# Weight sums of the branches' product pairs: from DRAM sums to VectorE sums in a two-layer recurrent trunk

## The chip, the cores and the metric

The kernel runs on one core of a Trainium2 chip. The metric is the device time of one execution in microseconds (us), the median of the runs taken. The engines that matter here are TensorE (PE in the profile, with its weight loads as PEld), VectorE (DVE), ScalarE (ACT), GpSimd (POOL) and SyncE (SP). SP only issues DMAs; ACT and POOL issue DMAs beside their arithmetic.

## The reference

The reference is a trunk of two layers over 512 frames of width 1024, all in float32. Each layer normalises x, projects it to about 12,300 columns, runs two branches (an mLSTM with four heads and a multi-scale retention with four heads, both chunkwise-recurrent), merges them under two sigmoid gates, and then adds a feed-forward block with a squared ReLU and a gated per-layer embedding. Cut to what the change touches:

```python
h = rmsnorm(x, norm1_g[i]);  z = h @ w_in[i] + b_in[i]     # q,k,v,o,i,f | rq,rk,rv,rg | gm,gr
rq4 = rope(rq, cos, sin);  rk4 = rope(rk, cos, sin) * R_DK ** -0.5
hr  = retention_chunkwise(rq4, rk4, rv, log_gamma)
y_r = silu(rg) * head_layernorm(hr)
merged = sigmoid(gm) * (y_m @ w_bm[i]) + sigmoid(gr) * (y_r @ w_br[i])
x = x + merged @ w_out[i]
x = x + square(relu(rmsnorm(x) @ w_ff1[i] + b_ff1[i])) @ w_ff2[i] + b_ff2[i]
x = x + sigmoid(rmsnorm(x) @ w_pe_gate[i]) * (p[i] @ w_pe[i])
```

## The kernel before

**Tiling.** Activations lie transposed in SBUF, 128 features by 512 frames to a tile. Every float32 operand is split into a high and a low part (`split`, L281 and L282: ScalarE writes the high part, VectorE subtracts it to get the low part), and TensorE multiplies high by high, high by low and low by high. A weight must therefore be loaded by SP, then pass through ScalarE, then through VectorE, before TensorE can use it.

**Units.** The work on weights is a fixed list of 314 units for the two layers (`unit_list`). 222 of them are whole: one 128x1024 block of weights of 512 KB, 24 matmuls of 512 columns. The other 92 are pairs (`PAIR`), which compute two output tiles by a seven-product scheme of the Strassen-Winograd kind in place of eight products: `P1` to `P7`, 12 matmuls of 256 columns each, run in the order P1, P5, P2, P6, P3, P7, and P4 only after the next unit has begun (`later`, `flush`). 22 pairs of a layer lie in the branches (rotary q and k, the gates rg, gr, and half of gm), 24 in the feed-forward block.

**Pieces of a pair.** A pair's weights are four quarters B11, B12, B21, B22 (128x512 each, 256 KB, given in `wpairs`) and four sums: t1 = B12 + B11, t3 = B12 + B22, t2 = t1 + B22 (three weights), t4 = t2 + B21 (four weights). They are loaded and split as four pieces: A = (B11, t1), B = (B21, t2), C = (B22, t3), D = (t4), the first three 128x1024, the last 128x512. A is used by P1 and P5, B by P2 and P6, C by P3 and P7, D by P4.

**Sums.** In this version the sums are all made in DRAM before they are needed. The pairs are grouped (24 groups, of four or two pairs), and each group has eight steps: for each of the four sums a DMA that copies the first addend, then a DMA that accumulates the second (`step`, L319, on POOL's queue; 1 MB a step for a group of four). There are 192 steps. `pace` gives each step a unit number from estimated unit times and four intervals in microseconds; `next_unit` issues all steps that are due when a unit begins, and each step carries a dependency on the last matmul written so far, so that it isn't issued before TensorE gets there.

**Loads.** SP loads the raw pieces (tile `wr`, L344 for pairs, L346 for whole units) into four buffers (`RAWS`), in the order in which they are used, about three pieces ahead. A buffer is free again when the piece in it is split. The split pieces A, B, C and the whole units share three pairs of buffers (tag `w`), D has a pair of its own, so a split waits as well until TensorE is done with an older piece. Program order is the priority; the framework's scheduler orders the instructions of each engine at build time by its own estimate of when each is ready, and each engine then runs its list strictly in order. A DMA that depends on nothing is put near the start of its engine's list.

**Evacuation.** The products of a pair accumulate in three PSUM banks (a, b, c). P6, P7 and P4 go on in bank a after ScalarE or VectorE have read what is there (`pair_tiles`, L446 after P1, L448 after P5, L452 after P6, L454 and L456 by VectorE after P3 and P7), and P3 goes on in bank c after L448. These reads stand in the same in-order lists as the splits.

**Rotation tables.** The cosine and sine tables (128x512 each) are loaded on ScalarE's queue (L1062), written in the program after the values of retention head 0, and used first by the rotary step of that head (L917 to L919), after four more units.

Of the kernel before, what the change touches and what calls it, by code (L numbers as in the profile page):

```python
# [38 lines left out]
OP = mybir.AluOpType  # L39
SYNC = mybir.DependencyInfo(mybir.DependencyClass.Sync, mybir.DependencyReason.DATA)  # L40
# [20 lines left out]

HALVED = (1, 2)

EVERY = (16.0, 7.2, 9.8, 11.3)


CQ, CK, CV, CO, CI, CF = 0, 1024, 2048, 3072, 4096, 4100
CRQ, CRK, CRV, CRG, CGM, CGR = 4104, 5128, 6152, 8200, 10248, 11272
# [25 lines left out]

PIECE = {"A": ("B11", "t1"), "B": ("B21", "t2"), "C": ("B22", "t3"), "D": ("t4",)}

GIVEN = ("B11", "B12", "B21", "B22")
MADE = {"t1": ("B12", "B11"), "t3": ("B12", "B22"), "t2": ("t1", "B22"), "t4": ("t2", "B21")}

READY = {"P1": 2, "P4": 2, "P5": 3, "P2": 4, "P6": 4, "P3": 5, "P7": 5}  # L100


def split_steps(k):

    return min(k + 1, 1), min(k, 48), min(max(k - 48, 0), 48), max(k - 96, 0)


def pace(units):

    at, t = [], 0.0  # L110
    for n, u in enumerate(units):
        while len(at) < 8 * len(groups()) and t >= sum(k * e for k, e in zip(split_steps(len(at)), EVERY)):
            at.append(n)
        t += 9.9 if u[0] == "PAIR" else 5.4
    return at


def groups():


    g = {}
    for i in range(L):
        def rqk(h):
            return [("w_in", 0, c + k * 256) for k in (h, h + 1) for c in (CRQ, CRK)]

        def rg(h):
            return [("w_in", 0, CRG + h * 512 + 256 * p) for p in range(4)]
# [103 lines left out]
def build(ctx, tc, ins, out):  # L231
# [1 line left out]
    ve, ac, gp, te = nc.vector, nc.scalar, nc.gpsimd, nc.tensor  # L233
    units = [u for i in range(L) for u in unit_list(i)]
    NU = len(units)
    due = pace(units)

    def pool(name, bufs, **kw):
        return ctx.enter_context(tc.tile_pool(name=name, bufs=bufs, **kw))
# [46 lines left out]
    for g, v in groups().items():  # L286
        index[g] = len(index)
        for x in GIVEN:
            given[g, x] = ins["wpairs"][k:k + len(v)]
            k += len(v)  # L290
        for x in MADE:
            sums[g, x] = tc.dram_tile([len(v), P, Q], F32, name=f"s{index[g]}{x}")

    def block(g, x):
# [5 lines left out]
    def sum_steps():  # L300

        first = lambda g: [(g, "t1", 0), (g, "t3", 0), (g, "t1", 1), (g, "t3", 1)]
        second = lambda g: [(g, "t2", 0), (g, "t2", 1), (g, "t4", 0), (g, "t4", 1)]
        gs = list(index)
        out = first(gs[0])
        for a, b in zip(gs, gs[1:]):
            for x, y in zip(second(a), first(b)):
                out += [x, y]
        return out + second(gs[-1])

    steps = sum_steps()
# [11 lines left out]
    def next_unit():  # L323
        n = at["unit"]
        at["unit"] += 1
        while at["step"] < len(steps) and due[at["step"]] <= n:
            step()
        return n


    order = [(n, x) for n, u in enumerate(units) for x in (PIECE if u[0] == "PAIR" else (0,))]
    place = {x: k for k, x in enumerate(order)}
    raws, pieces = {}, {}
    at = {"unit": 0, "prep": 0, "load": 0, "whole": 0, "step": 0}

    def fill_raws(most=RAWS):
        while at["load"] < len(order) and len(raws) < most:
            n, x = order[at["load"]]
            raws[n, x] = r = wpool.tile([P, UN], F32, name=f"wr{at['load']}", tag="wr", bufs=RAWS)
            if x:  # L340
                _, g, p = units[n]
                assert made[g] == 8, (g, made[g], at["unit"])
                for k, y in enumerate(PIECE[x]):
                    nc.sync.dma_start(r[:, k * Q:(k + 1) * Q], block(g, y)[p])  # L344
            else:
                nc.sync.dma_start(r, ins["wstream"][at["whole"]])  # L346
                at["whole"] += 1
            at["load"] += 1

    def prep_next():  # L350
        n, x = order[at["prep"]]
        at["prep"] += 1
        fill_raws()

        w = Q if x == "D" else UN
        pl = cur["last"] if n >= NU - LAST else wpool
        kw = {"tag": "d", "bufs": 2} if x == "D" else {"tag": "l", "bufs": 2 * LAST} if pl is not wpool else {
            "tag": "w", "bufs": 2 * PIECES}
        out_ = [pl.tile([P, w], F32R, name=f"w{a}{n}_{x}", **kw) for a in "hl"]
        split(raws.pop((n, x))[:, :w], *out_)  # L360
        pieces[n, x] = out_

    def ready(k):
# [414 lines left out]
    for i in range(L):  # L778
# [280 lines left out]

        trig = [cur["low"].tile([P, T], F32, name=f"l{i}{n}", tag="trig", bufs=2) for n in ("cos", "sin")]  # L1060
        for t, n in zip(trig, ("cos", "sin")):
            nc.scalar.dma_start(t, ins[n])  # L1062

        def bm_tile(c):
            if c < 4:
# [287 lines left out]
    cur["last"].release()  # L1353
    n3_pool.release()
    x_pool.release()
    assert at["unit"] == NU and at["prep"] == len(order) and not pieces and not raws and at["load"] == len(order) and at["step"] == len(steps)

# [110 lines left out]
```

## Time and profile before

| | us |
|---|---|
| runs | 2395.94, 2393.9, 2385.51 (median 2393.9) |
| the profiled execution | 2386.71 |
| its span, first to last instruction | 2385.0 |
| TensorE busy | 2344.7 |
| VectorE busy | 1654.2 |
| ScalarE busy | 1257.3 |
| GpSimd busy | 278.3 |

The granted TensorE clock is 0.995 over the span. The DMA queues moved 519.75 MB, of which 192.95 MB on POOL's queue. To read the profile: a group's line gives its source line, engine, operation, written and read tiles, count, busy time, mean duration in ns, and the idle time of the engine just before it with what ended it. In the list of waits, each line names who waited for whom and the total, the count and the longest in us. In the table of stretches each engine has its busy time and, in brackets, its instructions; the last three columns are the granted clock, the DMA engines' busy share and the GB/s that they moved. In the listing by time, the square brackets hold the idle time before the instruction and what ended it.

### The profile page before, as it was taken

Reading aid. Unit: us, or ns where it says so; the run is one execution under the profiler, and the core shown is the slowest. Engines: PE = TensorE matmul, PEld = TensorE weight load, DVE = VectorE, ACT = ScalarE, POOL = GpSimd, SP = SyncE. Lnnn points to the kernel's source line nnn. Section 1 sums busy time; section 2 is a strip of 40 time slices with the busy share of each in tenths; the row PEclk is TensorE's granted clock in tenths of the full one; section 3 lists DMA queues with packets and bytes.
Section 4 is the critical chain, followed back from the end, with each engine's and each line's share of the span. In section 5 each row is a group of like instructions: output and inputs, shape, how many; then the busy total and the mean of one; then the engine's idle time right before and its main releaser. Section 6 shows DMA issues by size and latency. Waiting matters only on the chain. (4 is left out here: it accounts for less than half of the span.)

```text
span 2385.0 us, 37288 instructions
## 1 busy us (share of the span) xinstructions
PE 2344.7 (98%) x14364; PEld 2099.3 (88%) x14364; DVE 1654.2 (69%) x2585; ACT 1257.3 (53%) x1864; POOL 278.3 (12%) x400
## 2 busy tenths in 40 slices
PE   9999989999999999999999999999999999999997
PEld 7788888998998899999887888898989888999996
DVE  6877466774666777777778775676737577777775
ACT  4765344553454656556547563444526456556563
POOL 3111101000001200001311110000000011000011
PEclk9999999999999999999999999999999999999998
DMA  7667799779799788977765567867786887895551
GB/s 227 172 195 197 216 272 261 248 203 268 198 282 301 231 262 235 285 229 220 209 192 141 178 163 225 247 193 205 211 248 188 276 251 214 271 246 184 174 158 42
DMA packets 197811, 519.75 MB, mean 218 GB/s; under 512 B 19313, under 2 KB 21745, under 8 KB 197633
## 3 DMA queue, kind: packets, MB, share of 16 engines
q1 hardware_dynamic: 130032, 292.84, 36.1%
q0 software_dynamic: 50176, 192.95, 34.5%
q10 hardware_dynamic: 17424, 31.59, 3.7%
q8 instruction: 112, 1.84, 0.3%
q14 instruction: 67, 0.54, 0.1%
HBM read 502.62 MB, written 207.62 MB: 298 GB/s over the span
## 5 line engine op out<-in xcount | busy, mean ns | idle before, releaser
L282 DVE TENSOR_TENSOR wl<-wr,wh 128x1024 fp32r<-128x1024 f32 x222 | 272.0, 1226 | 145.4 <-ACT wh L281 144.8
L281 ACT ACTIVATE wh<-wr 128x1024 fp32r<-128x1024 f32 x222 | 234.2, 1057 | 259.2 <-PE l0br L375 30.2
L281 ACT ACTIVATE wh_C<-wr 128x1024 fp32r<-128x1024 f32 x92 | 97.4, 1059 | 165.7 <-PE l1bm L375 13.1
L282 DVE TENSOR_TENSOR wl_D<-wr,wh_D 128x512 fp32r<-128x512 f32 x92 | 63.3, 688 | 128.2 <-ACT wh_D L281 121.2
L282 DVE TENSOR_TENSOR wl_C<-wr,wh_C 128x1024 fp32r<-128x1024 f32 x92 | 112.4, 1222 | 56.5 <-ACT wh_C L281 49.6
L281 ACT ACTIVATE wh_B<-wr 128x1024 fp32r<-128x1024 f32 x92 | 97.2, 1057 | 102.8 <-PE l1bm L375 5.5
L282 DVE TENSOR_TENSOR wl_B<-wr,wh_B 128x1024 fp32r<-128x1024 f32 x92 | 112.4, 1222 | 54.8 <-ACT wh_B L281 51.4
L282 DVE TENSOR_TENSOR wl_A<-wr,wh_A 128x1024 fp32r<-128x1024 f32 x92 | 113.9, 1238 | 40.1 <-ACT wh_A L281 38.6
L281 ACT ACTIVATE wh_D<-wr 128x512 fp32r<-128x512 f32 x92 | 57.9, 629 | 158.8 <-DMA wr<-s0t 20.1
L281 ACT ACTIVATE wh_A<-wr 128x1024 fp32r<-128x1024 f32 x92 | 97.0, 1055 | 48.3 <-DMA wr<-s0t 4.1
L374 PE MATMUL l0f<-l0n2h,wh 128*128 128x512 f32 x128 | 50.0, 391 | 0.0
L375 PE MATMUL l1f<-l1n2l,wh 128*128 128x512 f32 x128 | 50.0, 391 | 0.0
L374 PE MATMUL l1f<-l1n2h,wh 128*128 128x512 f32 x128 | 49.9, 390 | 0.0
L376 PE MATMUL l1f<-l1n2h,wl 128*128 128x512 f32 x128 | 49.9, 390 | 0.0
L376 PE MATMUL l0f<-l0n2h,wl 128*128 128x512 f32 x128 | 49.9, 390 | 0.0
L375 PE MATMUL l0f<-l0n2l,wh 128*128 128x512 f32 x128 | 49.9, 389 | 0.0
L376 PEld LDWEIGHTS l0f<-l0n2h,wl 128*128 128x128 f32 x128 | 24.0, 188 | 5.1
L375 PEld LDWEIGHTS l1f<-l1n2l,wh 128*128 128x128 f32 x128 | 24.0, 188 | 5.1 <-DVE l1n2l L522 0.4
L376 PEld LDWEIGHTS l1f<-l1n2h,wl 128*128 128x128 f32 x128 | 24.0, 188 | 5.0
L374 PEld LDWEIGHTS l1f<-l1n2h,wh 128*128 128x128 f32 x128 | 24.0, 188 | 4.8
L374 PEld LDWEIGHTS l0f<-l0n2h,wh 128*128 128x128 f32 x128 | 24.1, 188 | 4.7
L375 PEld LDWEIGHTS l0f<-l0n2l,wh 128*128 128x128 f32 x128 | 24.1, 188 | 4.7
(6357 smaller groups left out, 9002.2 us busy)
## 6 DMA issues: line engine op xcount, KB each, us to landing
wr<-wstream SPq DMA_DIRECT2D x222, 512.0 KB, 5.0
wr<-wpairs SPq DMA_DIRECT2D x276, 256.0 KB, 4.3
s0t<-wpairs POOLq DMA_DIRECT2D x6, 1024.0 KB, 10.3
s2t<-wpairs POOLq DMA_DIRECT2D x6, 1024.0 KB, 9.1
s3t<-wpairs POOLq DMA_DIRECT2D x6, 1024.0 KB, 10.0
s4t<-wpairs POOLq DMA_DIRECT2D x6, 1024.0 KB, 9.9
s5t<-wpairs POOLq DMA_DIRECT2D x6, 1024.0 KB, 9.7
s6t<-wpairs POOLq DMA_DIRECT2D x6, 1024.0 KB, 10.0
```

Of the source, the lines that this page charges most:

```text
L281: ac.activation(hi_ap, src, AF.Copy)
L282: ve.tensor_sub(lo_ap, src, hi_ap.bitcast(F32))
L374: te.matmul(o, sh, mh, start=first, stop=False)
L375: te.matmul(o, sh, ml, start=False, stop=False)
L376: cur["mm"] = te.matmul(o, sl, mh, start=False, stop=last)
```

## The change

For the twelve groups of the branches only t1 and t3 are still summed in DRAM (four steps a group). Their pairs load three raw pieces, in the order A = (B11, t1), C = (B22, t3), B = (B21), and no D. Before B is split, VectorE adds t1 (in A's raw tile) and B22 (in C's raw tile) into the free half of B's raw tile; this is t2. Before D is split, VectorE adds t2 to B21 in place; this is t4. A's raw tile is therefore held until the first sum, and B's until D is split. The feed-forward groups stay as they were. The steps go from 192 to 144, and the step k is due at a unit number worked out from k alone (17 units for 10 steps up to step 72, then 21 units for 10). The two rotation tables get a dependency on the last matmul written before them.

```diff
+LOADS = {True: {"A": ("B11", "t1"), "B": ("B21", "t2"), "C": ("B22", "t3"), "D": ("t4",)},
+         False: {"A": ("B11", "t1"), "C": ("B22", "t3"), "B": ("B21",)}}
...
-def split_steps(k):
-    return min(k + 1, 1), min(k, 48), min(max(k - 48, 0), 48), max(k - 96, 0)
-def pace(units):
...
+def due(k):
+    return 3 + 17 * min(k, 72) // 10 + 21 * max(k - 72, 0) // 10
+def in_dram(g):
+    return g[1][0] == "f"
...
-        for x in MADE:
+        for x in MADE if in_dram(g) else ("t1", "t3"):
             sums[g, x] = tc.dram_tile([len(v), P, Q], F32, name=f"s{index[g]}{x}")
...
-            for x, y in zip(second(a), first(b)):
-                out += [x, y]
+            if in_dram(a):
+                for x, y in zip(second(a), first(b)):
+                    out += [x, y]
+            else:
+                out += first(b)
...
-        while at["step"] < len(steps) and due[at["step"]] <= n:
+        while at["step"] < len(steps) and due(at["step"]) <= n:
             step()
...
+    loads = [(n, x) for n, u in enumerate(units) for x in (LOADS[in_dram(u[1])] if u[0] == "PAIR" else (0,))]
...
-        split(raws.pop((n, x))[:, :w], *out_)
+        f, l = slice(0, Q), slice(Q, 2 * Q)
+        if x in ("B", "C", "D") and not in_dram(units[n][1]):
+            b = raws[n, "B"]
+            if x == "B":
+                ve.tensor_tensor(b[:, l], raws.pop((n, "A"))[:, l], raws[n, "C"][:, f], OP.add)
+            elif x == "D":
+                ve.tensor_tensor(b[:, f], b[:, f], b[:, l], OP.add)
+            r = raws.pop((n, x)) if x == "C" else b
+            if x == "D":
+                del raws[n, "B"]
+        elif x == "A" and not in_dram(units[n][1]):
+            r = raws[n, x]
+        else:
+            r = raws.pop((n, x))
+        split(r[:, :w], *out_)
...
         for t, n in zip(trig, ("cos", "sin")):
-            nc.scalar.dma_start(t, ins[n])
+            dma = nc.scalar.dma_start(t, ins[n])
+            tc.add_manual_dep(dma.ins, cur["mm"].ins.name, SYNC, reason="not among the first loads")
```

More of the change, by code (lines that the diff above doesn't have):

```diff
@@ L62 @@
 HALVED = (1, 2)
-EVERY = (16.0, 7.2, 9.8, 11.3)
 CQ, CK, CV, CO, CI, CF = 0, 1024, 2048, 3072, 4096, 4100
@@ L100 @@
 READY = {"P1": 2, "P4": 2, "P5": 3, "P2": 4, "P6": 4, "P3": 5, "P7": 5}
-def split_steps(k):
-    return min(k + 1, 1), min(k, 48), min(max(k - 48, 0), 48), max(k - 96, 0)
-def pace(units):
[L110 to L115, printed above, removed]
+def due(k):
+    return 3 + 17 * min(k, 72) // 10 + 21 * max(k - 72, 0) // 10
+def in_dram(g):
+    return g[1][0] == "f"
 def groups():
@@ L235, in build @@
     NU = len(units)
-    due = pace(units)
     def pool(name, bufs, **kw):
@@ L336, in fill_raws @@
     def fill_raws(most=RAWS):
-        while at["load"] < len(order) and len(raws) < most:
-            n, x = order[at["load"]]
+        while at["load"] < len(loads) and len(raws) < most:
+            n, x = loads[at["load"]]
             raws[n, x] = r = wpool.tile([P, UN], F32, name=f"wr{at['load']}", tag="wr", bufs=RAWS)
@@ L341, in fill_raws @@
                 _, g, p = units[n]
-                assert made[g] == 8, (g, made[g], at["unit"])
-                for k, y in enumerate(PIECE[x]):
+                assert made[g] == (8 if in_dram(g) else 4), (g, made[g], at["unit"])
+                for k, y in enumerate(LOADS[in_dram(g)][x]):
                     nc.sync.dma_start(r[:, k * Q:(k + 1) * Q], block(g, y)[p])
@@ L1355, in build @@
     x_pool.release()
-    assert at["unit"] == NU and at["prep"] == len(order) and not pieces and not raws and at["load"] == len(order) and at["step"] == len(steps)
+    assert at["unit"] == NU and at["prep"] == len(order) and not pieces and not raws and at["load"] == len(loads) and at["step"] == len(steps)
 def _pack_units(a):
```

## The prediction

> **What bounds the kernel now.** I read the page first, then TensorE's waits, then the stretches in which these waits lie.
>
> ```profile
> span 2385.0 us, 37288 instructions
> ...
> PE 2344.7 (98%) x14364; PEld 2099.3 (88%) x14364; DVE 1654.2 (69%) x2585; ACT 1257.3 (53%) x1864; POOL 278.3 (12%) x400
> ...
> q0 software_dynamic: 50176, 192.95, 34.5%
> ```
>
> TensorE is the bound. Its matmuls stay the same, so the change can win only some of the 40.3 us in which TensorE is idle (2385.0 - 2344.7), and can lose by new waits without such a limit. q0, the queue of the DRAM sums, takes 34.5% of all DMA time. TensorE's waits that belong to the branches' pairs are these:
>
> ```profile
> PE l0r0brqa L423 <- ACT l0r0brqy L452: 2.0, 1, 2.0
> PE l1gr2c L423 <- ACT l1gr2y L448: 1.8, 1, 1.8
> PE l0bgm3a L423 <- ACT l0bgm3y L452: 1.6, 1, 1.6
> PE l0r0brqc L423 <- ACT l0r0brqy L448: 1.5, 1, 1.5
> PE l0bgm2c L423 <- ACT l0bgm2y L448: 1.3, 1, 1.3
> PE l1bgm2c L423 <- ACT l1bgm2y L448: 1.3, 1, 1.3
> PE l1gr3c L423 <- ACT l1gr3y L448: 0.9, 1, 0.9
> PE l0r0brqa L425 <- DVE wl_A L282: 0.7, 1, 0.7
> PE l1r2brqa L423 <- DVE l1r2brqy L456: 0.7, 1, 0.7
> ```
>
> They sum to 11.8 us. By stretches (start and end; busy time of PE, PEld, DVE, ACT, POOL; clock, DMA share, GB/s):
>
> ```profile
> 299.00:357.00 58.00, 51.17 (x372) 47.83 (x373) 36.06 (x50) 25.18 (x39) 4.51 (x7) 1.00 0.91 271
> 1477.00:1510.00 33.00, 31.57 (x253) 30.41 (x252) 25.55 (x37) 17.51 (x27) 2.68 (x3) 1.00 0.84 224
> 1865.00:1918.00 53.00, 50.17 (x327) 45.63 (x326) 30.92 (x42) 23.18 (x35) 2.98 (x4) 1.00 0.81 247
> 1040.00:1100.00 60.00, 59.83 (x417) 55.74 (x417) 44.69 (x65) 38.04 (x55) 3.63 (x5) 1.00 0.77 227
> ```
>
> The first branch pairs of layer 0 leave TensorE idle for 6.8 of 58 us with the DMA engines 91% busy; the fourth row, feed-forward pairs, leaves 0.2 of 60. What ScalarE waits for there:
>
> ```profile
> 309.05 1.06 ACT L281 ACTIVATE wh_B<-wr 128x1024 fp32r<-128x1024 f32 x1 [2.34 <-DMA wr<-s0t]
> 343.37 0.63 ACT L281 ACTIVATE wh_D<-wr 128x512 fp32r<-128x512 f32 x1 [6.45 <-DMA wr<-s1t]
> 353.83 1.06 ACT L281 ACTIVATE wh<-wr 128x1024 fp32r<-128x1024 f32 x1 [3.29 <-DMA wr<-wstream]
> 1884.45 0.63 ACT L281 ACTIVATE wh_D<-wr 128x512 fp32r<-128x512 f32 x1 [8.71 <-DMA wr<-s17t]
> ```
>
> In each row ScalarE stands in its in-order list before the split of a piece that hasn't landed, and the evacuations behind it (L448, L452) make TensorE wait. Over the whole kernel, of the loads at L344 (first row: waiter, us, times) and by landing time (rows below it):
>
> ```profile
>   ACT wh_D L281: 105.2, 20
> ...
> ```
> ```profile
> wr<-wpairs SPq DMA_DIRECT2D x276, 256.0 KB, 4.3
> wr<-s0t SPq DMA_DIRECT2D x16, 256.0 KB, 7.5
> wr<-s17t SPq DMA_DIRECT2D x16, 256.0 KB, 6.5
> wr<-s23t SPq DMA_DIRECT2D x16, 256.0 KB, 2.9
> ```
>
> D, the sum of four, is the piece that is waited for most.
>
> **The change part by part.** *Sums and loads taken away.* 192 steps become 144: for the 44 branch pairs four of eight DMAs over each 256 KB sum go, 44 x 4 x 0.262 MB = 46.1 MB of q0's 192.95, and with them 88 loads of 256 KB (23.1 MB) of t2 and t4 on SP's queue. POOL's list loses 48 issues, each with its wait on a matmul; what stands behind them on POOL comes no later. Bounds of what this wins: 0, if something else is late at the same places, and all that hangs on landings. That is, in 299 to 357 us, 2.0 + 1.6 + 1.5 + 0.7 = 5.8 us, and in 1865 to 1918 us, 1.8 + 0.9 = 2.7 us. The other waits (two of 1.3 and one of 0.7) aren't behind a DMA. The nearest rows are the two stretches with wh_D, where the awaited load is gone altogether, so I take most: -5.0 and -2.4.
>
> The landings by themselves, s0t's 7.5 against s23t's 2.9 us, are of one size and one queue; the first is read where the DMA engines are 91% busy, the second at the end, when q0 has no more sums. The Trainium skill, "DMA: Bandwidth & Descriptors", section "Issuing engines are not separate DMA queues", says that DMAs of all issuing engines run on the same 16 DMA engines and interleave. By that rule, fewer sums on POOL's queue also shorten SP's loads, and the sum stands as it is; were the queues separate, only the waits for D would go, of the two terms the -2.4 alone would stay, and the sum would be -2.2.
>
> *Pace.* The steps become due by units, about every 1.7 units. By the formula, every group's last step is still due well ahead of its first pair; the narrowest is layer 0's last feed-forward group, due at unit 129 and used from unit 145. No load waits for a sum: 0. If that cover were gone, SP would stop for a step.
>
> *Sums on VectorE.* Two additions of 128x512 a pair, 88 in all, of the kind and size of the second row:
>
> ```profile
> L282 DVE TENSOR_TENSOR wl_B<-wr,wh_B 128x1024 fp32r<-128x1024 f32 x92 | 112.4, 1222 | 54.8 <-ACT wh_B L281 51.4 <-DMA wr<-s16t 2.9 <-DMA wr<-s23t 0.2
> L282 DVE TENSOR_TENSOR wl_D<-wr,wh_D 128x512 fp32r<-128x512 f32 x92 | 63.3, 688 | 128.2 <-ACT wh_D L281 121.2 <-PE l1br L376 4.7
> ```
>
> 88 x 0.688 = 60.5 us of VectorE, 1.4 us a pair. Bounds: 0, if they lie in VectorE's idle time (128.2 us before wl_D alone), and +60.5, if each delays TensorE. They need raw tiles only, not the split buffers for which the splits wait, so they can run while a split waits. The place where they can't is the rotary step, where VectorE has no gap and ScalarE's evacuation waits behind it:
>
> ```profile
> 1489.72 0.69 DVE L282 TENSOR_TENSOR wl_D<-wr,wh_D 128x512 fp32r<-128x512 f32 x1 [1.23 <-ACT wh_D L281]
> ...
> 1492.32 0.68 DVE L919 TENSOR_TENSOR l1r0brqu<-l1r0brqu,l1r0brqw 128x512 f32<-128x512 f32 x1
> ```
> ```profile
> 1493.03 0.63 ACT L281 ACTIVATE l1r0qh<-l1r0brqu 128x512 fp32r<-128x512 f32 x1 [1.50 <-DVE l1r0brqu L919]
> 1493.57 0.37 ACT L448 ACTIVATE l1r0brky<-l1r0brkc 128x256 f32<-128x256 f32 x1
> ```
>
> An addition that falls into this chain puts L448, and P3 behind it, 0.69 us later. The gap of 1.23 us before wl_D takes t4, and rotary instructions go before the next pair's t2 by program order. I take one addition of 0.69 us at two places, one in each layer: +1.4.
>
> *Order of the loads.* B has half as much to load, but starts only when C's buffer is free; this is the second rival. Holding A's and B's raw tiles costs nothing while the loads land in about 4.3 us.
>
> *Rotation tables.* Two loads of 128x512 float32 (0.524 MB) leave the start:
>
> ```profile
> 1.22 0.45 ACTq L1062 DMA_DIRECT2D l0cos<-cos  x1
> ...
> 6.54 0.72 ACT L521 ACTIVATE l0n1h<-x,bc 128x512 fp32r<-128x512 f32 x1 [0.46 <-DMA x<-xT]
> ```
> ```profile
> 2.00:8.00 6.00, 6.00 (x39) 5.97 (x37) 1.89 (x2) 3.21 (x4) 3.61 (x21) 1.00 0.98 349
> ```
>
> The DMA engines are 98% busy at 349 GB/s while the first matmul's operands come in, so 0.524 MB are worth up to 1.5 us; at least 0, if x's conversion on ScalarE is the limit. I take -1.2, near the upper bound, as x is waited for. In their new place the wait is for the matmuls of the values of head 0, whose conversions on ScalarE stand ahead of it and wait for the same matmuls, so nothing behind it (splits, gate loads) comes later; four units lie before the first use.
>
> *Sum.* -5.0 - 2.4 + 1.4 - 1.2 = -7.2 us. The profiled execution took 2386.71 us, so 2379.5 for its like. The median of the runs, 2393.9, lies 7.2 us above that execution; on the median the forecast is 2386.7 us (0.30% less).
>
> **The rivals.** *More is won.* All nine waits go (11.8 us), the tables give 1.5 us, and the lighter DMA traffic takes some 2 us of short waits elsewhere: -15, 2379 us. For it: all these stretches have the DMA engines over 80% busy. Against it: three of the nine waits hang on no load.
>
> *B comes late, and it is slower.* B's load can start only when C's split is done:
>
> ```profile
> 658.58 1.23 DVE L282 TENSOR_TENSOR wl_C<-wr,wh_C 128x1024 fp32r<-128x1024 f32 x1 [0.55 <-ACT wh_C L281]
> ...
> 665.74 1.22 DVE L282 TENSOR_TENSOR wl_B<-wr,wh_B 128x1024 fp32r<-128x1024 f32 x1 [1.16 <-ACT wh_B L281]
> ...
> 667.75 0.42 DVE L456 TENSOR_TENSOR l0r3o1y<-l0r3o1a,l0r3o1y 128x256 f32<-128x256 f32 x1 [0.45 <-PE l0r3o1a L425]
> ```
>
> C's split ends at 659.8; B's ScalarE part, 1.06 us ahead of its VectorE part, is at 664.6. A landing of 4.3 us fits by 0.5 us; s0t's 7.5 us misses by 2.7 us, and then L456, which stands behind B's subtraction and which P4 waits for, slips. With 0.4 us of slack at L456 and the next pair's P1 in between, some 0.9 us reach TensorE: P1 is 12 matmuls, at the mean of the stretch from 1040 us (59.83 us for 417) 1.7 us, and as they are of the shorter kind I take 1.4. 18 branch pairs follow directly on another: 18 x 0.9 = 16 us, with an addition of 0.69 us in the chain at four more places about 19, less the tables' 1.2: 2411.5 us. It decides when most of these loads take over 5 us. Against it: the median of such loads is 4.3 us with the sums' traffic that is partly going.
>
> *The waits only move.* The places in which ScalarE now waits for D wait for B or C instead, and only the tables are won: -1 us, 2393.
>
> **How the numbers follow.** A measurement of this kernel can tell about 0.5% (12 us) from no change. The forecast, -2 to -12 us (2382 to 2392), has 0.40; more won 0.29; B late 0.25; only moved 0.06. So faster 0.29, same 0.40 + 0.06 = 0.46, slower 0.25. The range begins at 2371, the second case with the spread of the runs (2385.51 to 2395.94) below it, and ends at 2411, in the slower case; some 0.17 lies outside.
>
> **What would show it.** Right: no idle time of ScalarE before wh_D that ends with a DMA in the branches; s0t's loads landing in 5 us or less; DMA share in 299 to 357 us well under 0.91 and TensorE's idle time there about 2 us; the first real matmul about 1.2 us before 7.8 us. Wrong: TensorE waiting for evacuations (L448, L454, L456) behind an addition or behind wh_B; ScalarE idle before wh_B until the load of B21; a wait of ScalarE at the tables' DMA with splits behind it.

## The result, and the profile after

The changed kernel takes 2396.2 us (median of 21 runs, 2383.95 to 2404.62); the kernel before, run beside it, 2394.93 us (21 runs, 2383.49 to 2400.81). The ratio is 1.0006 with a 95% interval of 0.9992 to 1.0019: the change moves the time by less than can be told. The profiled execution of the changed kernel took 2383.95 us, 2.8 us less than that of before; both lie at the quick end of their runs, so these 2.8 us are no result, but the traces can be compared place by place.

From the page of the kernel after:

```profile
span 2382.2 us, 37036 instructions
...
PE 2340.4 (98%) x14364; PEld 2098.5 (88%) x14364; DVE 1707.3 (72%) x2673; ACT 1259.8 (53%) x1864; POOL 245.7 (10%) x352
...
q0 software_dynamic: 38144, 146.81, 26.9%
```

The work went where it was meant to go: q0 moves 46.1 MB less, VectorE is 53 us busier, POOL has 48 instructions less. TensorE's idle time, the span less its busy time, was 40.3 us and is 41.8.

TensorE's list of waits after (who waited for whom; total us, times, longest) shows new names in place of the old ones:

```profile
PE l1gr0a L436 <- DVE l1gr0y L469: 3.1, 1, 3.1
PE l1f L387 <- ACT l1n2h L534: 2.8, 1, 2.8
PE l0r3o1a L436 <- ACT l0r3o1y L465: 2.6, 1, 2.6
PE l0gr1a L436 <- DVE l0gr1y L469: 2.6, 1, 2.6
```

Of the nine waits shown of before, only those of l0bgm2c and l1bgm2c are left, with 0.6 us each. The stretches where the others lay, by the table of stretches of the kernel after (the second begins 8 us earlier, since the same work comes earlier):

```profile
299.00:357.00 58.00, 57.34 (x393) 52.86 (x393) 40.85 (x57) 26.95 (x41) 2.96 (x4) 1.00 0.74 210
...
1857.00:1910.00 53.00, 53.00 (x344) 48.48 (x343) 36.93 (x51) 25.38 (x37) 2.04 (x3) 1.00 0.80 232
```

The idle time of TensorE in the first is 0.7 us where it was 6.8, and the DMA share 0.74 where it was 0.91. So the gain that was looked for is there. To see where it goes, compare the first start of the same matmuls (tile by tile; the two numbers after the durations are the start of the first and of the last). Before:

```profile
L374 PE MATMUL l0r3a<-l0r3vh,l0r3ph x10: 389/389/476, 641.8 to 648.0; 128*128 128x512 f32 x10
...
L672 PE MATMUL l0r3ot<-ident,l0r3num x16: 272/272/273, 667.5 to 670.9; 128*128 128x128 f32 x16
...
L423 PE MATMUL l0gr2a<-l0xnh,wh_A x4: 278/283/283, 713.5 to 714.6; 128*128 128x256 f32 x4
...
L423 PE MATMUL l1gr1a<-l1xnh,wh_A x4: 277/283/283, 1865.4 to 1866.5; 128*128 128x256 f32 x4
```

And after:

```profile
L387 PE MATMUL l0r3a<-l0r3vh,l0r3ph x10: 389/389/478, 629.9 to 636.1; 128*128 128x512 f32 x10
...
L685 PE MATMUL l0r3ot<-ident,l0r3num x16: 271/272/273, 658.4 to 661.5; 128*128 128x128 f32 x16
...
L436 PE MATMUL l0gr2a<-l0xnh,wh_A x4: 278/283/283, 707.6 to 708.7; 128*128 128x256 f32 x4
...
L436 PE MATMUL l1gr1a<-l1xnh,wh_A x4: 277/283/283, 1860.8 to 1861.9; 128*128 128x256 f32 x4
```

At head 3 of the retention in layer 0 the kernel after is 11.9 us ahead (641.8 - 629.9), more than the whole forecast. Then it gives back: 9.1 us ahead at l0r3ot, 5.9 at l0gr2a. In layer 1 it is up to 9.6 us ahead in the branches, 4.6 at l1gr1a, 8.2 at the output projection, and 4.2 at the norm behind it. Early in the feed-forward block of layer 1 nothing of the lead is left (l1o01c starts at 2039.8 before and at 2040.0 after); the 2.8 us at the end are won behind the last branch pair. The four waits shown above have the same shape (at l1gr0 and l1f the awaited load is issued 3.5 and 2.8 us behind a step). The first two losses, in order of time on the engines' timeline after (start, duration, engine; in brackets the idle time before and what ended it):

```profile
646.08 1.01 POOL L317 DMA_DIRECT2D s9t<-wpairs  x1 [6.09 <-PE l0r3o0a L438]
...
647.93 0.33 SPq L343 DMA_DIRECT2D wr<-wpairs  x1
...
655.50 1.06 ACT L276 ACTIVATE wh_B<-wr 128x1024 fp32r<-128x1024 f32 x1 [4.15 <-DMA wr<-wpairs]
...
683.48 0.88 POOL L317 DMA_DIRECT2D s9t<-wpairs  x1 [11.75 <-PE l0br L389]
...
685.35 0.33 SPq L343 DMA_DIRECT2D wr<-wpairs  x1
...
694.05 0.69 DVE L363 TENSOR_TENSOR wr<-wr,wr 128x512 f32<-128x512 f32 x1 [5.29 <-DMA wr<-wpairs]
```

A step of a sum is issued by POOL, 1.9 us later SP issues a load, of B21 in the first case and of B22 in the second, and ScalarE (before the split of B) or VectorE (before the addition that makes t2) stands in its list until that load has landed. How long these two loads and the steps took from issue to landing, by the DMA view of these moments, and below them the medians of the whole kernel after:

```profile
s9t<-wpairs POOLq DMA_DIRECT2D x1, 1024.0 KB, 9.1
wr<-wpairs SPq DMA_DIRECT2D x1, 256.0 KB, 7.5
...
s9t<-wpairs POOLq DMA_DIRECT2D x1, 1024.0 KB, 10.3
...
wr<-wpairs SPq DMA_DIRECT2D x1, 256.0 KB, 8.6
...
wr<-wpairs SPq DMA_DIRECT2D x276, 256.0 KB, 3.2
...
wr<-s0t SPq DMA_DIRECT2D x8, 256.0 KB, 6.5
```

7.5 and 8.6 us against a median of 3.2. Counted over the trace, for the 256 KB loads whose landing it names (346 after, 334 before): those issued while a step was in flight (at least 1.5 us after its issue and 1 us before its landing) took a median of 5.5 us after (116 loads) and 6.3 us before (168 loads); those with no step in flight from their issue to their landing 3.0 us (172) and 2.9 us (70). The Trainium skill, "DMA: Bandwidth & Descriptors", section "Issuing engines are not separate DMA queues", says that DMAs started by any engine run on the same 16 DMA engines and interleave; these counts agree with it. The change makes the steps fewer, so fewer loads collide, but those that do still land after about 6 us, and there are new places where this is too late. VectorE's additions of t2 alone, over the whole kernel after (44 of them; busy us, mean ns; idle time before them and what ended it):

```profile
L363 DVE TENSOR_TENSOR wr<-wr,wr 128x512 f32<-128x512 f32 x44 | 30.1, 684 | 25.9 <-DMA wr<-wpairs 22.4
```

The additions themselves take what was forecast (684 ns); the 22.4 us in which VectorE stands before them, at 12 loads, were not in the forecast at all.

The losses are larger than the waits, because the granted TensorE clock drops behind most of them. The stretches after l0gr1's, l1gr0's and l1f's waits in the kernel after (columns as in the table of stretches):

```profile
696.10:699.50 3.40, 2.90 (x13) 2.90 (x14) 1.57 (x3) 0.72 (x1) 0.00 (x0) 0.50 1.04 414
1849.80:1853.20 3.40, 3.40 (x15) 3.21 (x15) 0.87 (x1) 1.29 (x3) 0.00 (x0) 0.50 0.72 199
1976.10:1982.90 6.80, 6.80 (x21) 5.57 (x21) 6.30 (x17) 2.67 (x4) 2.42 (x2) 0.50 0.89 176
```

Half the clock for 3.4, 3.4 and 6.8 us is up to 1.7, 1.7 and 3.4 us of work more, an estimate from these rows. With it the places add up: 2.6 + 1.7 = 4.3 us against a lead that falls from 9.9 (l0gr1a) to 5.9 us, 3.1 + 1.7 = 4.8 us against one that falls from 9.6 (l1gr0a) to 4.6. Behind the 2.6 us at l0r3o1a the clock stays at 1.00, and the lead falls by 2.8 us alone; why the clock drops behind one wait of 2.6 us and not behind the other isn't shown. Before has two such drops of 3.4 us ahead of the last 30 us (at 77.5 and 1296.1), none at these places.

### The profile page after: what moved, and what is told of

Its sections match the earlier page's. It is cut to its first block, busy times and chain, and to the rows that moved or that the text cites. A ratio compares the mean times of both kernels' runs of the same rounds, so it can differ in the third digit from the quotient of the medians.

```text
span 2382.2 us, 37036 instructions
## 1 busy us (share of the span) xinstructions
PE 2340.4 (98%) x14364; PEld 2098.5 (88%) x14364; DVE 1707.3 (72%) x2673; ACT 1259.8 (53%) x1864; POOL 245.7 (10%) x352
## 5 line engine op out<-in xcount | busy, mean ns | idle before, releaser
L277 DVE TENSOR_TENSOR wl_C<-wr,wh_C 128x1024 fp32r<-128x1024 f32 x92 | 112.3, 1221 | 39.8 <-ACT wh_C L276 33.1
L363 DVE TENSOR_TENSOR wr<-wr,wr 128x512 f32<-128x512 f32 x44 | 30.1, 684 | 25.9 <-DMA wr<-wpairs 22.4
L556 POOL TENSOR_TENSOR l1n3sum<-l1n3sum,l1n3sq 128x512 f32<-128x512 f32 x6 | 8.2, 1375 | 261.4 <-ACT l1n3sum L548 237.0
L365 DVE TENSOR_TENSOR wr<-wr 128x512 f32<-128x512 f32 x44 | 30.1, 684 | 0.4
```

Source lines behind the costliest of these rows:

```text
L277: ve.tensor_sub(lo_ap, src, hi_ap.bitcast(F32))
L363: ve.tensor_tensor(b[:, l], raws.pop((n, "A"))[:, l], raws[n, "C"][:, f], OP.add)
L365: ve.tensor_tensor(b[:, f], b[:, f], b[:, l], OP.add)
L556: gp.tensor_tensor(self.sum, self.sum, sq, OP.add)
```

## The experiments

**The theories.** Theory 1: what costs is a load that is issued while a step of a sum is in flight and meets a place with little slack; the additions are hidden. Theory 2: the additions in VectorE's in-order list eat what the lighter traffic gives. Where an expectation names another rival, it stands there.

### The tables alone

Before, with the rotation tables' dependency only:

```diff
-            nc.scalar.dma_start(t, ins[n])
+            dma = nc.scalar.dma_start(t, ins[n])
+            tc.add_manual_dep(dma.ins, cur["mm"].ins.name, SYNC, reason="not among the first loads")
```

> The kernel before with the rotation tables' dependency alone. Both theories: the first projection's matmuls start about 1 us earlier (13.7 us in place of 14.7), everything behind them is shifted by that and no more: ratio to before 0.9995, within noise. If the tables' new place costs something (512 KB loaded near 275 us, where the DMA engines are fully busy), the shift is used up by the first branch pairs: ratio 1.000 to 1.001.

Measured: 2395.18 us (11 runs) against 2392.14 of before (29 runs), ratio 1.0006 [0.999, 1.0022]. The first real matmul of this kernel, and below it the next product, l0m0z, in before and in this kernel (first and last start behind the durations):

```profile
6.96 0.48 PE L374 MATMUL l0if<-l0n1h,wh 128*128 128x512 f32 x1
...
L374 PE MATMUL l0m0z<-l0n1h,wh x32: 387/389/501, 14.7 to 38.3; 128*128 128x512 f32 x32
...
L374 PE MATMUL l0m0z<-l0n1h,wh x32: 387/389/504, 13.8 to 37.5; 128*128 128x512 f32 x32
```

The first starts 0.9 us before the 7.8 us of the kernel before, but in the kernel after at 8.19 us, later than before: the first matmul varies by about as much as this term. The next product tells more. It starts at 13.3 to 14.0 us in the eight traces with the moved tables and at 14.7 to 15.8 us in the six without, so the move wins about 1 us, as the expectation had it. In the time of whole runs 1 us can't be told.

### The sums on VectorE alone

After, but with the remaining steps at the units that the kernel before gives them, and the tables as before:

```diff
-def due(k):
-    return 3 + 17 * min(k, 72) // 10 + 21 * max(k - 72, 0) // 10
+def pace(units):
+    every = pace_all(units)
+    gs = list(groups())
+    kept = [True] * 4
+    for a, b in zip(gs, gs[1:]):
+        for x in range(4):
+            kept += [in_dram(a), True]
+    kept += [in_dram(gs[-1])] * 4
+    return [n for n, k in zip(every, kept) if k]
...
-            dma = nc.scalar.dma_start(t, ins[n])
-            tc.add_manual_dep(dma.ins, cur["mm"].ins.name, SYNC, reason="not among the first loads")
+            nc.scalar.dma_start(t, ins[n])
```

`pace_all` gives the units of before's 192 steps; those of the steps that are left are kept.

> The VectorE sums alone: t2 and t4 of the branches by VectorE, the steps that remain stay at the units at which the kernel before issues them, tables as before. Theory 1 (a load that is issued while a sum's 1 MB DMA is in flight lands 3 to 6 us late, and the waits are the places where this meets a tight piece): the branches' first pairs lose most of their waits, 299 to 357 us has under 3 us of TensorE idle time in place of 6.8, the whole is 4 to 10 us faster than before (ratio 0.996 to 0.998). Theory 2 (the additions in VectorE's in-order list eat the gain wherever the steps lie): ratio 0.999 to 1.001, with TensorE's waits behind L363 or L365.

Measured: 2401.1 us (12 runs), ratio 1.0022 [1.0007, 1.0038]: slower than before, by little, where theory 1 gave 0.996 to 0.998 and theory 2 0.999 to 1.001; both missed. The stretch from 299 to 357 us has 0.7 us of idle time, as theory 1 expected: the waits on D go by this part alone. But there are others, from TensorE's waits:

```profile
PE l1r0o1a L462 <- ACT l1r0o1y L491: 3.4, 1, 3.4
PE l0r3o1a L462 <- ACT l0r3o1y L491: 3.2, 1, 3.2
PE l1gr1a L462 <- DVE l1gr1y L495: 3.0, 1, 3.0
```

L491 is the evacuation behind the split of B. In six of the eight heads the second pair of the gate (o1, which follows directly on o0) waits here, 1.6 to 3.4 us. This is the rival "B comes late": with the steps where they were, the load of B21 often meets one. The pace of the kernel after takes most of these waits away and leaves one of size, l0r3o1a.

### The pace alone

Before, all 192 steps, due at a unit worked out from the step's number:

```diff
-def pace(units):
-    ...
+def due(k):
+    return 3 + 13 * min(k, 96) // 10 + 16 * max(k - 96, 0) // 10
```

> The kernel before with all 192 steps in DRAM but due by units (13 units for 10 steps in the first half, 16 for 10 in the second), tables as before. Theory 1: the first 350 us get fewer steps, so the waits there shrink to under 4 us, and others appear later where a step now meets a load: ratio 0.997 to 1.003. Theory 2: the pace plays no part, ratio 1.000 and the same waits at the same places.

Measured: 2396.36 us (12 runs), ratio 1.0011 [0.9995, 1.0026]. The waits move; those before 350 us don't shrink to under 4 us, as theory 1 had it, since l0r0brqa alone has 5.0. Among TensorE's largest are now:

```profile
PE l0r0brqa L411 <- ACT l0r0brqy L440: 5.0, 1, 5.0
...
PE l0wo L362 <- ACT l0mh L269: 3.0, 1, 3.0
```

None of the three parts wins by itself in the times of the runs.

### Both kernels without the sums' DMAs

After, and before, with no DRAM sums; a load that would read a sum reads a given quarter:

```diff
-        return given[g, x] if x in GIVEN else sums[g, x]
+        return given[g, x if x in GIVEN else {"t1": "B12", "t3": "B12", "t2": "B22", "t4": "B21"}[x]]
...
-        dma = gp.dma_start(flat(block(g, x)), flat(block(g, MADE[x][a])), max_dma_last_dim=4096, **kw)
-        tc.add_manual_dep(dma.ins, cur["mm"].ins.name, SYNC, reason="pace of the sums")
```

> The changed kernel with the sums in DRAM left out (every load that should read a sum reads a given quarter of the same size, so the pairs' products are of other weights); VectorE's additions stay. Theory 1: loads land in about 3 us throughout, no wait of ScalarE or VectorE for a pair's load over 1 us, and 10 to 18 us less than before (ratio 0.9925 to 0.996). Theory 2: the waits behind the additions stay, ratio 0.998 to 1.000.

> The kernel before with the sums in DRAM left out (the loads of sums read given quarters of the same size, so the pairs' products are of other weights); beside the changed kernel without sums (2361 us) it prices VectorE's additions by themselves, with no sum's DMA in flight. Theory 1 (the waits come from loads that meet a sum's DMA, additions are hidden): within 4 us of that one, 2358 to 2366 us, ratio 0.985 to 0.989. Theory 2 (the additions cost): 10 us or more under it, ratio 0.981 or less. Theory 3 (loading t2 and t4 on SP's queue costs even without sums): 2370 us or more.

Measured: after without sums 2361.23 us (4 runs, 2356.9 to 2361.45), ratio to before 0.985 [0.9831, 0.987]; before without sums 2366.52 us (6 runs, 2364.33 to 2367.14), ratio 0.9886 [0.9867, 0.9905]. From the pages, after and before, both without sums:

```profile
PE 2334.4 (99%) x14364; PEld 2095.3 (89%) x14364; DVE 1709.9 (72%) x2673; ACT 1258.9 (53%) x1864; POOL 129.7 (5%) x208
...
PE 2335.5 (99%) x14364; PEld 2094.0 (89%) x14364; DVE 1658.7 (70%) x2585; ACT 1259.3 (53%) x1864; POOL 127.7 (5%) x208
```

Three things follow. The additions are no price that could be seen: with the same 88 additions, and 88 loads less, after is the quicker of the two by 5.3 us in the medians (2.9 us in the profiled spans, 2359.7 and 2362.6), so theory 2 falls. What the additions cost and what the loads win was not measured apart.

The steps' DMAs, those of the feed-forward pairs included, cost some 27 us in before and more than 30 in after, more than theory 1 gave (10 to 18 us), though on the computing side they pass through POOL's list alone. That is far more than the 11.8 us of waits that the profile of before showed in the branches. The two profiled executions of before, with and without sums, show where the rest lies: of the 22.4 us between their spans (2385.0 and 2362.6), TensorE's idle time makes up 13.2 (40.3 against 27.1), and 9.2 are longer busy time for the same 14364 matmuls (2344.7 against 2335.5). The drops of the granted clock behind waits are a part of that: without sums there is none between 20 and 2330 us in either kernel.

Without the sums the runs also agree within 5 us (4 and 6 runs); those of before and after spread over 17 and 21 (21 runs each). A part of a step's cost thus comes and goes from run to run.

### Steps clear of the pairs, and steps on the pairs

After, with its 144 steps due only at units that are no pair and have none directly behind them:

```diff
-def due(k):
-    return 3 + 17 * min(k, 72) // 10 + 21 * max(k - 72, 0) // 10
+def clear(units):
+    pair = [u[0] == "PAIR" for u in units] + [True]
+    at = [n for n in range(3, len(units)) if not pair[n] and not pair[n + 1]]
+    return [at[int(k / 0.9 if k < 72 else 80 + (k - 72) / 0.75)] for k in range(144)]
```

> The changed kernel with its 144 steps due only at units that are no pair and have no pair behind them (0.9 a unit up to step 72, then 0.75), packets as before. Theory 1: sums meet the loads of whole units, which have over 10 us to spare, and seldom a piece: fewer TensorE waits in the pairs, 10 to 25 us less than before, ratio 0.990 to 0.996. Against: in the whole units the DMA engines are over 90% busy, and loads run late there too: ratio 0.999 to 1.004.

Then the opposite: the same 144 steps at the same mean rate, but those that fall into the branches and the feed-forward block moved to the units which are a pair or stand directly before one:

```diff
+    d = [at[int(k / 0.9 if k < 72 else 80 + (k - 72) / 0.75)] for k in range(144)]
+    for lo, hi in ((44, 148), (201, 306)):
+        ks = [k for k in range(144) if lo <= d[k] < hi]
+        to = [n for n in range(lo, hi) if (pair[n] or pair[n + 1]) and n <= d[ks[-1]]]
+        for j, k in enumerate(ks):
+            d[k] = to[j * len(to) // len(ks)]
```

> After, with the same 144 steps at the same mean rate as the kernel that kept them clear of pairs (2384.8 us), but in the branches and the feed-forward they are put on the opposite units: those that are a pair or stand directly before one. Theory 1 (a load of a pair that is issued while a sum is in flight lands 3 us late and becomes a wait): the waits at first and second pairs come back and multiply, 2400 to 2415 us, slower than after. Theory 2b (what helped the clear kernel was its rate, a little quicker at first and slower later, and not where the steps stand): 2385 within 4 us, as with the clear steps.

Measured: clear of the pairs 2384.8 us (12 runs, 2382.79 to 2390.21) against 2393.75 of before, ratio 0.9965 [0.9949, 0.998]; on the pairs 2406.76 us (6 runs, 2403.27 to 2413.39) against 2395.51, ratio 1.0051 [1.0031, 1.0071]. The clear steps win 9 us, just less than the 10 to 25 of theory 1. The additions of t2 in the kernel with clear steps:

```profile
L366 DVE TENSOR_TENSOR wr<-wr,wr 128x512 f32<-128x512 f32 x44 | 30.1, 683 | 9.8 <-DMA wr<-wpairs 9.3
```

The same, and the splits of B, with the steps on the pairs:

```profile
L285 ACT ACTIVATE wh_B<-wr 128x1024 fp32r<-128x1024 f32 x92 | 97.4, 1059 | 141.0 <-DMA wr<-wpairs 25.4 <-PE l1bm L397 6.5 <-PE l0bm L397 5.3
...
L372 DVE TENSOR_TENSOR wr<-wr,wr 128x512 f32<-128x512 f32 x44 | 30.1, 684 | 31.6 <-DMA wr<-wpairs 25.5 <-issue 5.7
```

And TensorE's waits with the steps on the pairs:

```profile
PE l1gr1a L445 <- DVE l1gr1y L478: 4.1, 1, 4.1
...
PE l1r2o1a L445 <- ACT l1r2o1y L474: 2.9, 1, 2.9
PE l0r1o1a L445 <- ACT l0r1o1y L474: 2.9, 1, 2.9
```

VectorE's standing before t2 goes 9.3, 22.4, 25.5 us from clear over after to on the pairs. The two ends have the same sums, additions, loads and mean rate of steps: where the steps stand is worth some 21 us (1.0051 - 0.9965 of 2395). The 2400 to 2415 us that theory 1 gave for the steps on the pairs held, and theory 2b's 2385 fell. The kernel with clear steps is faster than both kernels compared here.

Two limits. The number of loads under a step, counted as above, is 61 with clear steps, 116 in after and 111 on the pairs: it halves from after to clear, but it doesn't rise on the pairs. What rises there is ScalarE's standing before the split of B for a load, 25.4 us against 6.4 in after and none with clear steps, so it matters which load is hit. And the profiled executions of after and of the clear kernel differ by 0.6 us only (2382.2 and 2381.6), as that of after is a quick one: where the 11 us between their medians lie, these traces don't show. Crowding of the steps doesn't follow the times: a step is issued while another has more than 1 us to go 59 times in the clear kernel, 11 in after, 41 on the pairs.

### Before with clear steps

Does the clear placing need the additions by VectorE? Before, with all its 192 steps on such units, five steps to four units up to step 100, then one to one:

```diff
-def pace(units):
-    ...
+def clear(units):
+    pair = [u[0] == "PAIR" for u in units] + [True]
+    at = [n for n in range(3, len(units)) if not pair[n] and not pair[n + 1]]
+    return [at[int(k / 1.25 if k < 100 else 84 + (k - 100))] for k in range(192)]
```

> Before, with its 192 steps (all four sums in DRAM, nothing added by VectorE) put on the units that are neither a pair nor directly before one, five steps to four such units up to step 100 and one a unit from there. It tells whether the clear placing needs the additions by VectorE. Theory 1 (the collision of sums and pair loads is the cost, whoever adds): faster than before by 4 to 9 us, 2385 to 2390 us. Rival (a quarter fewer steps is what makes room for the clear placing): with 192 steps the units are so full that loads next to them collide all the same, 2392 to 2400 us.

Measured: 2451.8 us (5 runs), ratio 1.025 [1.0226, 1.0273], worse than either expectation. The stretch of the matrix-memory branch (start and end; busy time of PE, PEld, DVE, ACT, POOL; clock, DMA share, GB/s), before:

```profile
130.00:310.00 180.00, 176.06 (x867) 148.55 (x865) 116.78 (x218) 93.03 (x151) 28.99 (x59) 1.00 0.75 212
```

With clear steps:

```profile
130.00:310.00 180.00, 163.05 (x745) 135.46 (x744) 108.19 (x209) 86.04 (x144) 35.61 (x68) 0.94 0.92 250
```

And the waits of all engines in that stretch:

```profile
POOL s4t L311 <- issue: 27.4, 5, 8.7
POOL s3t L311 <- issue: 23.3, 3, 9.6
...
DVE l0m1num L658 <- POOL l0m1hv L886: 10.8, 1, 10.8
```

Steps that come quicker than they drain hold POOL at their issue (the profile names no releaser there), and POOL's own work for the matrix memory, which VectorE waits for, comes late behind them. TensorE idles 17 us there instead of 4, and its matmuls run at a granted clock of 0.94. Over the whole span, 39.8 of the 62.6 us that the span grows by are idle time of TensorE and 22.8 longer busy time for the same matmuls. How the loss divides between POOL's list and the DMA engines at 92% was not separated, and so the question is answered by counting alone: the list has 190 clear units, fewer than the 192 steps, and at one step or a little more to a unit the sums of layer 0's last feed-forward group would come after their first use. The 144 steps of the changed kernel fit.

### Smaller steps and smaller packets

If a 4 KB packet of a sum holds up the 2 KB packets of a load, smaller packets should help. First, each step in four DMAs (two for the groups of two pairs), limited to 1 KB packets, in after and in before:

```diff
-        dma = gp.dma_start(flat(block(g, x)), flat(block(g, MADE[x][a])), max_dma_last_dim=4096, **kw)
+        o, s = block(g, x), block(g, MADE[x][a])
+        w = max(1, o.shape[0] // 4)
+        for k in range(0, o.shape[0], w):
+            dma = gp.dma_start(flat(o[k:k + w]), flat(s[k:k + w]), max_dma_last_dim=1024, **kw)
```

> The changed kernel with each step in four DMAs of a quarter each, in packets of 1 KB in place of 4 KB, at the same units; the same bytes. Theory 1 with the DMA engines taking turns by packet: a piece's load is 8 packets of 2 KB on an engine, each behind one packet of the sum; with packets a quarter as long its delay falls from some 3 us to under 1.5 us, and half or more of the 35 us between the changed kernel and the one without sums comes back: ratio to before 0.988 to 0.995. If a load instead stands behind all of a sum that was issued ahead of it: no change, ratio 0.999 to 1.002. If short packets make the sums themselves much slower (over 14 us in place of 8.4): loads are late for longer, ratio over 1.002.

> The same packets of 1 KB in the kernel before, all four sums in DRAM. Theory 1 with turns by packet: it gains as the changed kernel does, ratio 0.988 to 0.995, as its loads meet sums more often still (168 piece loads issued while a sum was in flight against 116). If the gain of short packets is in VectorE's list only: ratio 1.000.

Measured: 2540.41 us, ratio 1.0615 [1.059, 1.0641], and 2819.62 us, ratio 1.1783 [1.1753, 1.1813]. The loads did land earlier under a step (a median of 3.9 us instead of 5.5 in after, counted as above), and it helped nothing. But the limit took hold only in the accumulating half of the DMAs. POOL's queue in after with this edit, during its first copies (24 to 42 us, first row) and its first accumulations (44 to 56 us, second row): packets, of which 112 and 32 have 4 bytes, then MB and share:

```profile
q0 software_dynamic: 601, 2.00, 28.8%
...
q0 software_dynamic: 544, 0.52, 32.1%
```

The copies still move in packets of 4096 bytes, 17,920 of them over the trace at a median of 159 ns; an accumulating packet takes 327 ns with 4 KB, 178 with 2 KB and 102 with 1 KB. The waits of all engines from 835 to 870 us in after with 1 KB packets, and one of TensorE there:

```profile
ACT l0n2sq L550 <- POOL l0n2sum L558: 26.6, 1, 26.6
DVE l0ns1u L493 <- ACT l0nsr L1176: 26.6, 1, 26.6
POOL s10t L320 <- issue: 12.9, 4, 4.4
...
PE l0wo L389 <- ACT wh L276: 18.7, 1, 18.7
```

POOL stands 3 to 4 us before each of these quarter steps with no releaser named, and an addition of the norm that stands behind them in POOL's list (L558) keeps ScalarE waiting for 26.6 us; VectorE and TensorE follow. Summed over POOL's waits, its step issues stand so for 1167 us (338 of 560), against 7 us (one) in after and 123 us (13) in before. Between the profiled spans of after with and without this edit (2544.6 and 2382.2 us) TensorE's idle time makes up 114.2 us, and 48.2 are longer busy time, at a mean granted clock of 0.964 against 0.994.

To divide the number of issues from the size of the packets, two DMAs a step (one for the groups of two pairs), once with 4 KB packets and once with 2 KB (2048 in the last line; again only the accumulating DMAs follow):

```diff
-        dma = gp.dma_start(flat(block(g, x)), flat(block(g, MADE[x][a])), max_dma_last_dim=4096, **kw)
+        w = max(1, o.shape[0] // 2)
+        for k in range(0, o.shape[0], w):
+            dma = gp.dma_start(flat(o[k:k + w]), flat(s[k:k + w]), max_dma_last_dim=4096, **kw)
```

> After, with each step of a sum issued as two DMAs of 512 KB by POOL instead of one of 1 MB; the packets stay 4 KB. It prices the number of POOL's issues by itself, to divide the 144 us that four issues a step with 1 KB packets cost (2540.4 us). Theory 1a (that loss came from POOL's list: each issue occupies POOL, and the norms' and denominators' work on POOL, and what waits for it, comes late): 144 more issues, a third of the 432 more there, cost about a third of the loss, 30 to 50 us, 2425 to 2445 us. Theory 1b (the loss came from the small packets at the DMA engines): the packets are the same, the time stays at 2396 within 6 us.

> The same two DMAs a step, with 2 KB packets, as large as those of the piece loads. Against the run with 4 KB packets it prices the packet alone. Theory 1 (a load shares the DMA engines with the sum packet by packet, and a 4 KB packet of a sum holds an engine four times as long as a 2 KB packet of a load): loads under sums land earlier, so fewer waits, 5 to 15 us less than with 4 KB halves. Theory 1b (small packets cost the DMA engines time): 10 to 60 us more than with 4 KB halves.

Measured: 4 KB halves 2386.93 us (10 runs, 2382.97 to 2391.15), ratio 0.9967 [0.9956, 0.9979]; 2 KB halves 2385.94 us (9 runs, 2380.78 to 2390.49), ratio 0.9964 [0.995, 0.9977]. Both expectations for the 4 KB halves missed: 144 more issues on POOL cost nothing, and the time fell by some 9 us instead of staying. The number of issues is thus not what holds POOL, up to 288 of them: with the steps due at the same units, it stands longer the more packets the queue has, 0 us with 40,448, 510 us with 58,368 and 1167 us with 98,560. With 2 KB packets it stands at 91 of 288 issues, yet without harm. Both expectations for the 2 KB packets missed too: the packet's size alone is worth nothing here: 1.0 us between the two, within their spread, though loads under a step land after 4.8 instead of 5.8 us. The Trainium skill, "DMA: Bandwidth & Descriptors", section "SWDGE vs HWDGE vs iDMA", says that a DMA engine takes turns between its queues; the shorter landings with 2 KB packets fit that, the time does not show it.

Why halves help stays open. A half lands after 5.8 us instead of 8.4 for a whole step, but a load under it takes no less than under a whole one (5.8 and 5.5 us), and the profiled executions of after and of the halves, both quick ones, show nearly the same waits. What differs is that the long runs of after, up to 2404.62 us, don't occur among those of the halves.

## Why the prediction was right, and where it was not

The time, 2396.2 us, lies in the range, 9.5 us above the value, and "the same within 0.5%" was the likeliest case. That the range holds it is owed to its width of 40 us, which takes in three of the four cases: the gain that was forecast, a ratio of 0.9970, lies outside the measured 0.9992 to 1.0019. The mechanism of the gain was right, the sum left out what takes it back. The four terms, one by one:

- **-5.0 in 299 to 357 us: right.** The waits on D went, TensorE's idle time there fell by 6.2 us and the DMA share from 0.91 to 0.74; the lead grows by 5.0 us, from 4.2 at l0r0brqc (300.4 against 296.2) to 9.2 at l0bgm3a (346.3 against 337.1). That there are 4.2 us before the first branch pair, where only the tables were to win, was not forecast. Of the marks named, only the landing of s0t missed: 6.5 us, not 5 or less, with no wait of TensorE to show for it in that stretch.
- **-2.4 in layer 1's gr pairs: right about the waits, wrong about the place.** The two waits are gone, and 1857 to 1910 us has no idle time. But the pair just ahead, l1gr0, has a new one of 3.1 us.
- **+1.4 for additions: the term that failed.** It priced the additions by their duration and asked only whether they lie in VectorE's gaps. It said that they need raw tiles only and "can run while a split waits", and didn't ask what stands behind them when the raw tile is late: t2 needs C's load, which now comes right before B's, and the evacuations that VectorE makes for the same pair (L469 and the like) stand behind the addition. What the runs showed in its place: the durations cost nothing that could be seen (2361.23 without sums against 2366.52), the standing before them 22.4 us of VectorE's time, of which 3.1 + 2.6 us reach TensorE at l1gr0 and l0gr1 in the profile, and behind each of them the clock drops for 3.4 us, which no term had. One of the signs named for "wrong", TensorE waiting for evacuations behind an addition or behind wh_B, is what the trace shows.
- **-1.2 for the tables: right by the traces, too small for the times.** The second product starts about 1 us earlier wherever the tables are moved; the first real matmul, which was the named mark, varies by as much and shows nothing. Alone the tables give a ratio of 1.0006 [0.999, 1.0022].

The rival **"B comes late"** had the right mechanism and the wrong extent. It was to strike at 18 pairs (by the unit list, 26 follow directly on another) if most of these loads took over 5 us. Most don't (3.2 us in the median), but those under a step do (5.5). So it strikes where a step happens to stand: at one pair in after (2.6 us), at six in the kernel with the sums alone. **"The waits only move"** came nearest to what happened, and had only 0.06: the places changed from the wait for D to waits for B, for t2, and, at the start of the feed-forward block of layer 1, for a D that is still summed in DRAM. Together with the clock behind them they gave back all of the 11.9 us won by 641.8 us; 2.8 came again later.

The rule of the Trainium skill that was weighed against separate queues ("DMA: Bandwidth & Descriptors", "Issuing engines are not separate DMA queues") held by the landings above. But it was used one-sidedly: that fewer sums shorten the loads. By it the 144 steps that are left lengthen the loads too, and that was the larger matter.

## What to carry to other kernels

When a change takes a late piece away, look for the piece that is then the last, and ask which DMA in the background is in flight at the moment its load is issued: the median landing time says little when landings have two values, 3 and 6 us here. Background DMAs are best placed by what they collide with: the same 144 steps cost some 21 us more beside the tight loads than clear of them. Take a background stream away altogether for one run; it gives its whole price (27 us here), of which the waits found in the branches showed less than half. And price a wait of TensorE by more than its length where the granted clock drops behind it, as it did here for 3.4 or 6.8 us.

## What the runs showed of the hardware

- A 256 KB load on SP's queue lands after 2.9 to 3.0 us with no step in flight and after 5.5 to 6.3 us when one of POOL's 1 MB DRAM-to-DRAM steps is in flight (medians of after and before).
- The granted TensorE clock went to 0.50 for 3.4 us behind waits of 2.6 us (l0gr1a) and 3.1 us (l1gr0a) and for 6.8 us behind one of 2.8 us (l1f), but stayed at 1.00 behind 2.6 us at l0r3o1a.
- The run times spread over 17 to 21 us in before and after (21 runs each), over 5 us or less without the steps (4 and 6 runs).
- On POOL's queue an accumulating packet of 4 KB took 327 ns of a DMA engine, a copying one 159 ns.
- Four DMAs a step, the accumulating ones with 1 KB packets, cost 6% and 18%, with POOL standing 1167 us at its issues in the first and the loads landing earlier (3.9 us under a step, 5.5 in after); two DMAs a step, with 4 KB or 2 KB packets, are 0.3% faster than the kernel before.
- How long the steps hold POOL at their issue doesn't give the loss by itself: 510 us of such standing cost nothing with 2 KB halves, some 290 us (123 in before) went with a loss of 56 us where the matrix memory's work stood behind it.
